# Hybrid decoder step on one core: first weight blocks on a second queue, fewer unread products, and the third block's transposes moved

## The chip, the cores and the metric

The kernel runs on one core of a Trainium2 chip. The metric is the device time of one launch in microseconds. A core has a matrix engine (TensorE, PE in the profile; its weight loads are listed apart as PEld), a vector engine (VectorE, DVE), a scalar engine (ScalarE, ACT), GpSimd (POOL) and SyncE (SP), each with its own instruction stream. In this kernel SP issues most transfers; ScalarE and GpSimd issue some.

## The reference, cut to what matters

The reference is one inference step of a hybrid decoder layer (Mamba-2 and gated linear attention side by side, cross-attention into 256 memory tokens, a convolutional feed-forward part). It serves a prompt of 256 tokens and 8 samples of 4 tokens. The change concerns the first thing the kernel computes, the memory keys and values of the prompt:

```python
def _mem_kv(mem, norm_mem, w_ck, w_cv):
    mn = _rmsnorm(mem, norm_mem)                    # mem: 256 rows of 2048
    k = (mn @ w_ck).reshape(Bsz, N_MEM, CROSS_HEADS, CROSS_HEAD_DIM)
    v = (mn @ w_cv).reshape(Bsz, N_MEM, CROSS_HEADS, CROSS_HEAD_DIM)
```

The first stage of the kernel is one quarter of the first product: the keys of head 0, `mn @ w_ck[:, 0:512]`, a 256 x 2048 matrix times a 2048 x 512 one. The row factor of the norm (`mrs`) is applied at the end of the product, so the stage only has to scale by the gains `norm_mem` before it multiplies.

## The kernel before, in words

The contraction over 2048 is cut into 16 blocks of 128 (`KT`). Every operand is split into a high and a low float32r half, and a product is made of three matmul terms: high x high, low x high, high x low. A weight block of 128 x 512 (256 KB, tile `raw`) is loaded by `wload` (L108), and `wsplit` (L100) makes `whi` with a ScalarE cast (L103) and `wlo` with a VectorE subtraction (L105). Six `raw` tiles are in rotation, five pairs of halves.

The memory rows are loaded two blocks at a time by `mem_load` (L290, 256 KB into `mt`). `mem_prep` (L296) turns one block: two TensorE transposes (L300), then `split_from` (L195), in which ScalarE multiplies by the gain and writes `mn_hi` (L197) and VectorE writes `mn_lo` (L198). The gains come as a row `mrow`, loaded on ScalarE's queue (L285), are turned by one transpose (L374) and copied to `gmem` (L375).

`prep_mem` (L371) calls `mem_prep`, and for every odd block squares one 128 x 512 piece of the rows on ScalarE (L384), with its sum read out, for the row factor; block 15 has two such pieces. So on ScalarE the order within an odd block is gain, square, cast; within an even block gain, cast.

`mem_proj` (L326) puts it together. Its generator `feed` issues the loads of a pair of blocks, prepares each block and splits its weights. Before the loop, `ready` is filled with blocks 0 and 1. In the loop, block `kk` is multiplied with six matmuls of 512 columns (L348, L349 for each half of the rows, then L352), and then `ready` is filled again: with two blocks after block 0, with one after each other block. So the transposes of blocks 2 and 3 stand between the products of blocks 0 and 1, and from then on the transposes of block k+3 stand behind the products of block k.

Two groups of products of a matrix of ones, which nobody reads, stand on TensorE: nine ahead of the stage (L389), six after the transposes of block 1 (L379).

Within this stage the order on TensorE, ScalarE, VectorE and SP is the program's, written out by `tc.manual_schedule` (L385). The rest of the program is ordered by a planner that simulates time (L42); it may move an instruction forward into free places, which is how an instruction of line 533 (`acol`, the exponential of a small vector) and the copies of line 455 (`dcol`) stand among those of this stage. `tc.keep_in_program_order` pins an instruction.

After this stage the same `mem_proj` runs for other heads without `prep`, woven with the preparation of x (L501).

Of the kernel before, what the change touches and what calls it, by code (L numbers as in the profile page):

```python
# [11 lines left out]
ACT = mybir.ActivationFunctionType  # L12
# [4 lines left out]
P = 128  # L17
# [25 lines left out]
def hybrid_step(ctx: ExitStack, tc: tile.TileContext, I: dict, O: list):  # L43
    ctx.enter_context(tc.block(schedule_with_timeline_sim=True))
    nc = tc.nc
    (y_p, y_s, o_pconv, o_pssd, o_pgla, o_pffn, o_pmk, o_pmv, o_sconv, o_sssd, o_sgla, o_sffn) = O
    V, S, G = nc.vector, nc.scalar, nc.gpsimd
# [13 lines left out]
    def acc_tiles(n):  # L61

        turn[0] += 1
        return [ps.tile([P, 512], F32, tag=f"acc{turn[0] % 2}", bufs=2, name="acc") for _ in range(n)]

    def mm_tile():
        return ps.tile([P, 512], F32, tag="mm", bufs=3, name="mm")
# [23 lines left out]
    dcol = const.tile([P, KT], F32, name="dcol")  # L91
    dtb = const.tile([32, 1], F32, name="dtb")
    alog = const.tile([32, 1], F32, name="alog")

    def vec(name):
        o, n = vofs[name]
        return vcol[:, o:o + n]


    def wsplit(raw):  # L100

        hi = wp.tile(list(raw.shape), F32R, tag="whi", bufs=WB, name="whi")
        S.copy(hi, raw)  # L103
        lo = wp.tile(list(raw.shape), F32R, tag="wlo", bufs=WB, name="wlo")
        V.tensor_tensor(lo, raw, hi, ALU.subtract)  # L105
        return hi, lo

    def wload(src):  # L108
        raw = wp.tile([P, src.shape[1], src.shape[2]], F32, tag="raw", bufs=RB, name="raw")
        nc.sync.dma_start(out=raw, in_=src)  # L110
        return raw

    late = []
# [57 lines left out]
    def run(*gens):  # L171
        for g in gens:
            for _ in g:
                pass
# [105 lines left out]
    with pool("p0") as p0:  # L280
# [1 line left out]
        mn_lo = p0.tile([P, KT, SEQ], F32R, name="mn_lo")  # L282
        vrow = p0.tile([P, P], F32, name="vrow")
        mrow = p0.tile([KT, P], F32, name="mrow")
        S.dma_start(out=mrow, in_=I["norm_mem"].rearrange("(t p) -> t p", p=P))  # L285
        S.preload_act_table_set(LNEXP)
        S.copy(epsc[:, 2:3], epsc[:, 0:1])
        mt = p0.tile([P, 9, 512], F32, tag="rows", name="mt")[:, 0:8].rearrange("p (i q) d -> p i (q d)", i=2)
# [1 line left out]
        def mem_load(k0):  # L290
            cs = slice(k0 * P, (k0 + 2) * P)
            nc.sync.dma_start(out=mt[:, :, cs], in_=I["mem_prompt"][0, :, cs].rearrange("(i p) c -> p i c", p=P))
# [33 lines left out]
        def mem_proj(w, hd, dst, prep=None, hold=None):  # L326

            def feed():
                for k0 in range(0, KT, 2):
                    if prep is not None:  # L330
                        mem_load(k0)
                    raws = [wload(w[k * P:(k + 1) * P, 512 * hd:512 * hd + 512].rearrange("(k p) n -> p k n", p=P))
                            for k in (k0, k0 + 1)]
                    for k in range(2):
                        if prep is not None:
                            prep(k0 + k)
                        yield wsplit(raws.pop(0))

            accs = acc_tiles(2)
            ws = feed()  # L340
            ready = [next(ws) for _ in range(2)] if prep is not None else []
            for kk in range(KT):
                if prep is None:
                    ready.append(next(ws))
                hi, lo = ready.pop(0)
                for m in range(2):
                    ms_ = slice(m * P, (m + 1) * P)
                    MM(accs[m], mn_hi[:, kk, ms_], hi[:, 0, :], start=(kk == 0), stop=False)  # L348
                    MM(accs[m], mn_lo[:, kk, ms_], hi[:, 0, :], start=False, stop=False)  # L349
                for m in range(2):  # L350
                    ms_ = slice(m * P, (m + 1) * P)
                    MM(accs[m], mn_hi[:, kk, ms_], lo[:, 0, :], start=False, stop=(kk == KT - 1))  # L352
                if prep is not None:
                    ready += [w_ for w_ in (next(ws, None) for _ in range(2 if kk == 0 else 1)) if w_]
                if turning and next(turning[0], STOP) is STOP:
                    turning.pop(0)
                yield

            def rows():
                t = p0.tile([P, 2, 512], F32, tag="mp", bufs=2, name="mp")  # L360
                for m in range(2):
                    S.activation(t[:, m, :], accs[m], ACT.Identity, scale=mrs[:, m:m + 1])
                G.dma_start(out=dst[0, :, hd, :].rearrange("(m p) d -> p m d", p=P), in_=t)
                if dst is o_pmk:
                    turning.append(key_turn(hd, t))
            if hold is None:
                rows()
            else:
                hold.append(rows)

        def prep_mem(kk):  # L371
            if kk == 0:
                a = mm_tile()
                TR(a[:, 0:KT], mrow, ident[0:KT, 0:KT])  # L374
                V.tensor_copy(gmem, a[:, 0:KT])  # L375
            mem_prep(kk)
            if kk == 1:
                for _ in range(6):
                    MM(wm[:, 0:P], ones, ones, start=True, stop=True)  # L379
            for n in range(kk // 2 - 1 if kk % 2 else 8, kk // 2 + kk // (KT - 1)):  # L380
                if n >= 0:
                    sq = p0.tile([P, 512], F32, name="junk")
                    i, q = n % 2, n // 2
                    S.activation(sq, mt[:, i, q * 512:(q + 1) * 512], ACT.Square, accum_out=mss[:, i, q:q + 1])  # L384
        with tc.manual_schedule(engines={mybir.EngineType.PE, mybir.EngineType.Activation, mybir.EngineType.DVE,  # L385
                                        mybir.EngineType.SP}):
            wm = mm_tile()
            for _ in range(9):
                MM(wm[:, 0:P], ones, ones, start=True, stop=True)  # L389
            run(mem_proj(I["w_ck"], 0, o_pmk, prep_mem, held))  # L390

# [14 lines left out]
        drow = p0.tile([P, 2 * KT], F32, name="drow")  # L406
# [15 lines left out]
        def x_norm():  # L422
            ss = p0.tile([P, 9], F32, name="ss")

            def square(b):
                junk = p0.tile([P, 512], F32, name="junk")
                tc.keep_in_program_order(S.activation(junk, xrow[:, b, :], ACT.Square, accum_out=ss[:, b:b + 1]))
                tc.keep_in_program_order(
                    V.transpose(xT[:, :, 32 * b:32 * b + 32], xrow[:, b, :].rearrange("p (x j) -> p j x", j=KT)))

            for step in range(37):
                if step in (5, 9, 15, 21, 27):
                    x_load((step - 3) // 6)
                if step == 3:

                    V.tensor_reduce(mrs, mss, AX.X, ALU.add)
                    S.activation(mrs, mrs, ACT.Ln, scale=1.0 / D, bias=epsc[:, 0:1])
                    S.activation(mrs, mrs, ACT.Exp, scale=-0.5)
                if step == 6:
                    held.pop()()  # L440
                if step % 3 == 0 and step >= 12:
                    square(step // 3 - 5 if step > 12 else 8)
                yield
            yield
            a = mm_tile()
            TR(a[:, 0:r], vrow[0:r, :], ident[0:r, 0:r])
            TR(a[:, 128:224], crow, ident[0:96, 0:96])
            yield
            V.tensor_copy(vcol[:, 0:r], a[:, 0:r])
            V.tensor_scalar(scw, a[:, 128:224], 0.5, None, ALU.mult)  # L450
            ob, nb_ = vofs["ssd_conv_b"]
            V.tensor_scalar(vcol[:, ob:ob + nb_], vcol[:, ob:ob + nb_], 0.5, None, ALU.mult)
            V.tensor_scalar(rg, vec("gla_norm"), 0.5, None, ALU.mult)
            for e in range(2):
                V.tensor_copy(dcol[64 * e:64 * e + 64, :],
                              drow[64 * e:64 * e + 64, :].rearrange("p (t e) -> p e t", e=2)[:, e, :])
            yield

            dg = p0.tile([P, 9, NS], F32, name="dg")
            V.tensor_tensor(dg, fold4.unsqueeze(1).to_broadcast([P, 9, NS]), ss.unsqueeze(2).to_broadcast([P, 9, NS]), ALU.mult)  # L460
            yield
            a = mm_tile()
            MM(a[:, 0:T], ones, dg.rearrange("p c t -> p (c t)"), start=True, stop=True)
            S.activation(rtok, a[:, 0:T], ACT.Ln, scale=1.0 / D, bias=epsc[:, 0:1])
            S.activation(rtok, rtok, ACT.Exp, scale=-0.5)
# [45 lines left out]
        acol = p0.tile([32, 1], F32, name="acol")  # L511
# [18 lines left out]
        run(proj_w(dt_load, 112, X, KT, dt_cons))  # L530

        def dt_prep():
            S.activation(acol, alog, ACT.Exp)
            S.activation(dte, dtx, ACT.Abs)
            S.activation(dte, dte, ACT.Exp, scale=-1.0)
            S.activation(dte, dte, ACT.Ln, bias=1.0)
# [1191 lines left out]
    for i in range(5):  # L1728
        src = I["ffn_conv_w"][i] if i < 3 else I["ffn_conv_b"] if i == 3 else I["norm_final"]
# [266 lines left out]
```

## Time and profile before

| what | value |
|---|---|
| median of 3 runs | 2477.01 us (2476.76 to 2479.82) |
| the profiled execution, its own time | 2480.01 us |
| its span, first to last instruction | 2478.3 us |
| TensorE busy | 2464.7 us, 99% of the span |
| VectorE, ScalarE, GpSimd busy | 1774.8, 1354.7, 439.4 us |
| moved by DMA | 530.77 MB, 214 GB/s on average |

The first stage takes the first 33 us or so of this span. A row of a time line has the start, the duration, the engine, the line and operation, the tile written and the tiles read, and a count; in brackets stands how long the engine idled before it and what released it. "SPq" and "ACTq" are issues of transfers from SP and ScalarE. Durations of matmuls overlap, since they are pipelined: the distance between starts is their rate.

### The profile page before, as it was taken

The page shows a single profiled execution, that of the slowest core. Times are in us where ns is not written, and L with a number is a line of the kernel's source. Part 1 is how long each engine was busy: PE and PEld are TensorE (multiplying, and loading weights), DVE is VectorE, ACT ScalarE, POOL GpSimd, SP SyncE. Part 2 cuts the span into 40 slices and gives each one's busy share as a digit, 9 for nine tenths or more (in the row PEclk, how much of TensorE's full clock was granted, in tenths as well). Part 3 has the DMA queues.
Part 4 walks back from the last instruction along what each step waited for, and adds up shares of the span by engine and source line. Part 5 has one row for each costly group of instructions (what it writes and reads, how often), then busy time and mean ns, then how long its engine had stood idle before and what let it go on. Part 6 is the DMA issues. An engine that isn't in the chain of part 4 may idle for free.

```text
span 2478.3 us, 52123 instructions
## 1 busy us (share of the span) xinstructions
PE 2464.7 (99%) x18738; PEld 2385.7 (96%) x18738; DVE 1774.8 (72%) x3804; ACT 1354.7 (55%) x2781; POOL 439.4 (18%) x798
## 2 busy tenths in 40 slices
PE   9999999999999999999999999999999999999998
PEld 7889999999999999999999998999999999999998
DVE  6866778796877666777666676667777676776766
ACT  6765657646464655544455554565545454554545
POOL 3103144252111010110111122402101001010012
PEclk9999999999999999999999999999999999999999
DMA  8878687777769685877777698656555555555555
GB/s 259 258 237 236 175 261 210 224 224 227 218 210 297 198 262 184 244 254 221 233 232 256 199 355 308 198 165 174 168 172 171 171 168 177 167 174 169 170 172 168
DMA packets 457652, 530.77 MB, mean 214 GB/s; under 512 B 40316, under 2 KB 403676, under 8 KB 457360
## 3 DMA queue, kind: packets, MB, share of 16 engines
q1 hardware_dynamic: 420272, 422.39, 56.4%
q0 software_dynamic: 37088, 105.03, 13.2%
q8 instruction: 147, 2.41, 0.4%
q14 instruction: 113, 0.93, 0.1%
q10 hardware_dynamic: 32, 0.01, 0.0%
HBM read 476.41 MB, written 50.86 MB: 213 GB/s over the span
## 4 chain that ended last, share of the span: by engine, by line
PE 96%; DMA 2%; DVE 1%; POOL 1%; ACT 0%; issue 0%; SPq 0%; DVEq 0%; POOLq 0%; ACTq 0%
PE acc L149 27%; PE acc L148 27%; PE acc L153 27%; PE acc L348 2%; PE acc L352 2%; PE acc L349 2%; DMA raw<-in_w_in_dram 1%; POOL sqr L777 1%; PE mm L1260 1%; PE la L1251 1%; PE la L1603 1%; PE la L1661 1%; PE mm L1215 0%; DMA vc<-in_cache_mem_v_dram 0%; PE la L926 0%
## 5 line engine op out<-in xcount | busy, mean ns | idle before, releaser
L103 ACT CAST whi<-raw 128x512 fp32r<-128x512 f32 x1464 | 898.3, 618 | 951.4 <-PE acc L149 805.1
L105 DVE TENSOR_TENSOR wlo<-raw,whi 128x512 fp32r<-128x512 f32 x1464 | 994.3, 686 | 532.5 <-ACT whi L103 522.4
L149 PE MATMUL acc<-xn,whi 128*128 128x288 f32 (+1 forms) x1936 | 540.8, 295 | 0.0
L148 PE MATMUL acc<-xn,whi 128*128 128x288 f32 (+1 forms) x1936 | 539.6, 294 | 0.2 <-ACT whi L103 0.2
L153 PE MATMUL acc<-xn,wlo 128*128 128x288 f32 (+1 forms) x1936 | 407.9, 293 | 0.0
L149 PE MATMUL acc<-hf,whi 128*128 128x288 f32 x1408 | 393.2, 296 | 0.0
L148 PE MATMUL acc<-hf,whi 128*128 128x288 f32 x1408 | 388.6, 292 | 0.0
L148 PEld LDWEIGHTS acc<-xn,whi 128*128 128x128 f32 (+1 forms) x1936 | 363.4, 188 | 5.6 <-issue 3.5
L149 PEld LDWEIGHTS acc<-xn,whi 128*128 128x128 f32 (+1 forms) x1936 | 363.7, 188 | 3.1
L153 PEld LDWEIGHTS acc<-xn,wlo 128*128 128x128 f32 (+1 forms) x1936 | 309.8, 188 | 0.5 <-DVE wlo L105 0.2
L153 PE MATMUL acc<-hf,wlo 128*128 128x288 f32 x1408 | 294.5, 290 | 0.0
L149 PEld LDWEIGHTS acc<-hf,whi 128*128 128x128 f32 x1408 | 264.5, 188 | 0.0
L148 PEld LDWEIGHTS acc<-hf,whi 128*128 128x128 f32 x1408 | 264.0, 188 | 0.0
L153 PEld LDWEIGHTS acc<-hf,wlo 128*128 128x128 f32 x1408 | 226.3, 188 | 0.1
L149 PE MATMUL acc<-pr,whi 128*128 128x288 f32 x704 | 196.5, 295 | 0.0
L148 PE MATMUL acc<-pr,whi 128*128 128x288 f32 x704 | 194.7, 293 | 0.0
L1777 POOL COPY fsp<-fst 128x16 f32<-128x16 f32 x88 | 36.2, 413 | 653.6 <-DVE av L1789 371.3
L153 PE MATMUL acc<-pr,wlo 128*128 128x288 f32 x704 | 147.3, 290 | 0.0
L148 PE MATMUL acc<-un,whi 128*128 128x288 f32 x512 | 143.1, 295 | 0.3 <-DVE ma L1031 0.3
L149 PE MATMUL acc<-un,whi 128*128 128x288 f32 x512 | 143.0, 295 | 0.0
L149 PEld LDWEIGHTS acc<-pr,whi 128*128 128x128 f32 x704 | 132.3, 188 | 0.0
L148 PEld LDWEIGHTS acc<-pr,whi 128*128 128x128 f32 x704 | 132.0, 188 | 0.0
(564 smaller groups left out, 4316.6 us busy)
## 6 DMA issues: line engine op xcount, KB each, us to landing
raw<-in_w_in_dram SPq DMA_DIRECT2D x480, 256.0 KB, 3.9
raw<-in_w_up_dram SPq DMA_DIRECT2D x352, 256.0 KB, 2.8
raw<-in_w_down_dram SPq DMA_DIRECT2D x176, 256.0 KB, 2.9
raw<-in_w_ck_dram SPq DMA_DIRECT2D x64, 256.0 KB, 5.2
raw<-in_w_cv_dram SPq DMA_DIRECT2D x64, 256.0 KB, 4.5
raw<-in_w_ssd_out_dram SPq DMA_DIRECT2D x64, 256.0 KB, 3.5
sin<-in_state_gla_dram POOLq DMA_DIRECT2D x32, 512.0 KB, 6.4
out_dram<-sin SPq DMA_DIRECT2D x32, 512.0 KB, 3.7
```

The lines of the kernel that those rows point to most:

```text
L103: S.copy(hi, raw)
L105: V.tensor_tensor(lo, raw, hi, ALU.subtract)
L148: MM(a, hi[:, k, cs], xh, start=(k0 + s0 + k == 0), stop=False)
L149: MM(a, hi[:, k, cs], xl, start=False, stop=False)
L153: MM(a, lo[:, k, cs], xh, start=False, stop=(k0 + s0 + k == nk - 1))
L348: MM(accs[m], mn_hi[:, kk, ms_], hi[:, 0, :], start=(kk == 0), stop=False)
L349: MM(accs[m], mn_lo[:, kk, ms_], hi[:, 0, :], start=False, stop=False)
L352: MM(accs[m], mn_hi[:, kk, ms_], lo[:, 0, :], start=False, stop=(kk == KT - 1))
L777: tc.keep_in_program_order(G.dma_start(out=sq_[32 * i:32 * i + 32].rearrange("p (r d) -> p r d", d=32), in_=rows[i]))
L1251: MM(osa[NS * j:NS * j + NS, :], qdm[:, k, b, :], sins[b][:, k, :], start=False, stop=(q == 1 and k == 0))
L1260: MM(a, kb[:, k * P:(k + 1) * P], vst, start=True, stop=True)
L1777: G.tensor_copy(sp[:, :, 0:2], st.rearrange("p (b k) -> p b k", k=2))
```

## The change

Six edits, all in what runs first or is pinned:

1. `wload` takes an engine. The first two weight blocks of `w_ck` are loaded by ScalarE's queue (`first`), at the place where the gain row was loaded.
2. The gain row is loaded by SP, after the first memory rows.
3. The memory rows of blocks 2 and 3 are loaded directly after it, ahead of all other weight blocks; the later order is unchanged.
4. The unread products are five and two instead of nine and six.
5. The pair of blocks that was prepared after the products of block 0 is not prepared there. Block 2 is prepared within block 1, after the first two of its matmuls, and block 3 at the end of block 1; from then on one block after each block, as before.
6. The copies to `dcol` and the exponential to `acol` are pinned to the program's order.

```diff
-    def wload(src):
+    def wload(src, eng=None):
         raw = wp.tile([P, src.shape[1], src.shape[2]], F32, tag="raw", bufs=RB, name="raw")
-        nc.sync.dma_start(out=raw, in_=src)
+        (eng or nc.sync).dma_start(out=raw, in_=src)
...
-        S.dma_start(out=mrow, in_=I["norm_mem"].rearrange("(t p) -> t p", p=P))
+        first = [wload(I["w_ck"][k * P:(k + 1) * P, 0:512].rearrange("(k p) n -> p k n", p=P), S) for k in range(2)]
...
                 for k0 in range(0, KT, 2):
-                    if prep is not None:
+                    if prep is not None and k0 != 2:
                         mem_load(k0)
-                    raws = [wload(w[k * P:(k + 1) * P, 512 * hd:512 * hd + 512].rearrange("(k p) n -> p k n", p=P))
-                            for k in (k0, k0 + 1)]
+                    if prep is not None and k0 == 0:
+                        nc.sync.dma_start(out=mrow, in_=I["norm_mem"].rearrange("(t p) -> t p", p=P))
+                        mem_load(2)
+                        raws = first
+                    else:
+                        raws = [wload(w[k * P:(k + 1) * P, 512 * hd:512 * hd + 512].rearrange("(k p) n -> p k n", p=P))
+                                for k in (k0, k0 + 1)]
...
                     MM(accs[m], mn_lo[:, kk, ms_], hi[:, 0, :], start=False, stop=False)
+                    if prep is not None and kk == 1 and m == 0:
+                        ready.append(next(ws))
...
-                if prep is not None:
-                    ready += [w_ for w_ in (next(ws, None) for _ in range(2 if kk == 0 else 1)) if w_]
+                if prep is not None and kk:
+                    ready += [w_ for w_ in (next(ws, None),) if w_]
...
             if kk == 1:
-                for _ in range(6):
+                for _ in range(2):
                     MM(wm[:, 0:P], ones, ones, start=True, stop=True)
...
-            for _ in range(9):
+            for _ in range(5):
                 MM(wm[:, 0:P], ones, ones, start=True, stop=True)
...
-                V.tensor_copy(dcol[64 * e:64 * e + 64, :],
-                              drow[64 * e:64 * e + 64, :].rearrange("p (t e) -> p e t", e=2)[:, e, :])
+                tc.keep_in_program_order(V.tensor_copy(
+                    dcol[64 * e:64 * e + 64, :], drow[64 * e:64 * e + 64, :].rearrange("p (t e) -> p e t", e=2)[:, e, :]))
...
-            S.activation(acol, alog, ACT.Exp)
+            tc.keep_in_program_order(S.activation(acol, alog, ACT.Exp))
```

## Prediction

> **What bounds the kernel now.** I read the page first, then the waits of TensorE, then the time lines of TensorE, ScalarE and the SP queue over the first 33 us, because the change touches nothing later.
>
> ```profile
> span 2478.3 us, 52123 instructions
> PE 2464.7 (99%) x18738; PEld 2385.7 (96%) x18738; DVE 1774.8 (72%) x3804; ACT 1354.7 (55%) x2781; POOL 439.4 (18%) x798
> ...
> PE 96%; DMA 2%; DVE 1%; POOL 1%; ACT 0%; issue 0%; SPq 0%; DVEq 0%; POOLq 0%; ACTq 0%
> ...
> PE la L1661 <- DMA vc<-in_cache_mem_v_dram: 1.3, 1, 1.3
> ...
> PE mm L300 <- DMA mt<-in_mem_prompt_dram: 0.6, 1, 0.6
> ```
>
> TensorE is busy for 99% of the span and makes 96% of the chain that ended last, so a microsecond won or lost on TensorE at the beginning is a microsecond at the end. The list of TensorE's waits (total, times, longest) shows how little is left to win: the longest one, far behind the change, and one for the memory rows. What the beginning can also win is time in which TensorE is busy with products nobody reads; the busy share doesn't tell those apart, the time line does (start, duration, count).
>
> ```profile
> 1.13 3.83 PE L389 MATMUL mm<-ones 128*128 128x128 f32 x18 [1.13 <-DVE epsc L78]
> 4.90 0.23 PE L374 MATMUL mm<-ident,mrow 16*128 16x16 f32 x1
> 5.06 0.44 PE L300 MATMUL mm<-ident,mt 128*128 128x128 f32 x2
> ...
> 5.55 1.50 PE L379 MATMUL mm<-ones 128*128 128x128 f32 x12
> 6.81 0.48 PE L348 MATMUL acc<-whi,mn_hi 128*128 128x512 f32 x1
> ...
> 9.05 0.44 PE L300 MATMUL mm<-ident,mt 128*128 128x128 f32 x2 [0.60 <-DMA mt<-in_mem_prompt_dram]
> ...
> 9.46 0.48 PE L348 MATMUL acc<-whi,mn_hi 128*128 128x512 f32 x1
> ...
> 11.32 0.48 PE L348 MATMUL acc<-whi,mn_hi 128*128 128x512 f32 x1
> ```
>
> Nine unread products (18 instructions) run from 1.13; the transposes of blocks 0 and 1 from 5.06; six more unread products from 5.55; the products of block 0 from 6.81. Then TensorE waits for the second load of memory rows, transposes blocks 2 and 3 at 9.05, and does the products of block 1 from 9.46 and of block 2 from 11.32. From there it doesn't wait in this stage. The measure of the new beginning is therefore the start of block 2's products, now 11.32.
>
> **The first part: the new beginning.** Who lets block 0 and block 2 start is seen on the queues.
>
> ```profile
> 0.82 0.46 SPq L292 DMA_DIRECT2D mt<-in_mem_prompt_dram  x1
> 1.34 0.93 SPq L110 DMA_DIRECT2D raw<-in_w_ck_dram  x2
> ...
> 2.31 6.69 DMA mt<-in_mem_prompt_dram
> ...
> 0.81 0.44 ACTq L285 DMA_DIRECT2D mrow<-in_norm_mem_dram  x1
> 1.29 1.28 ACT L286 ACT_TABLE_LOAD   x1 [1.29 <-PEq L1984]
> ...
> 5.53 0.47 ACT L197 ACTIVATE mn_hi<-mm,gmem 128x256 fp32r<-128x256 f32 x1 [2.76 <-PE mm L300]
> 5.91 0.61 ACT L103 CAST whi<-raw 128x512 fp32r<-128x512 f32 x1
> ...
> 9.89 0.61 ACT L103 CAST whi<-raw 128x512 fp32r<-128x512 f32 x1
> ...
> 3.00:4.00 1.00, 1.00 (x6) 1.00 (x6) 1.00 (x2) 0.00 (x0) 1.00 (x5) 1.00 1.11 323
> ```
>
> Unread products. Eighteen instructions become ten, twelve become four. The first ten end at about 1.13 + 10 x 0.21 = 3.3 (3.83 / 18 = 0.21 each), so TensorE is free for the transposes from 3.3 instead of 4.90. But the transposes need the gains (mrow) and the first rows, and the trace doesn't say when these land, only that both were there by 4.90 and 5.06. The change puts mrow behind the rows on SP and lets the first weight block run beside the rows. The last row above is a stretch of 1 us in which all queues moved 323 GB/s: one more transfer of 262 KB served in between delays the rows by at most 0.8 us. So the transposes of block 0 start between 3.3 (all landed early) and 5.06 + 0.8 = 5.9. I take 5.4, half of the delay on top of 5.06: four 256 KB transfers took until 9.00, and no row shows an early landing. From there ScalarE decides: the first transposes start at 5.06 and the cast of the first weight block ends at 5.91 + 0.61 = 6.52, 1.46 us later. The products of block 0 start at 5.4 + 1.5 = 6.9. Two unread products (4 instructions of (6.81 - 5.55) / 12 = 0.11, 0.44 in all) fit in between and cost nothing. Block 0 takes six products, 1.4 us (below), so block 1 starts at 8.3 and, after its first two products, the transposes of block 2 come at 8.8.
>
> Loads. The rows of blocks 2 and 3 (issued at 2.31, landed at 9.00) are now SP's third transfer, about 0.5 us earlier. The bytes ahead of and beside them stay the same, four times 256 KB. I take 8.5 for the landing (bounds 7.5 and 9.0); at 8.8 nobody waits for them, at 9.0 it costs 0.2.
>
> ScalarE issues two transfers instead of one before its table load, 0.5 us more; its next work is due at 5.53, the table load ends at 2.57, so this is covered by over 2 us. The later weight blocks are issued two places earlier on SP; nothing is queued behind them that TensorE needs sooner.
>
> Block 2's products need its cast. From the transposes at 9.05 to the end of that cast at 9.89 + 0.61 = 10.50 were 1.45 us; from 8.8 that gives 10.25, and TensorE's own path (four products, one transpose pair) gives 10.1. So block 2 starts at 10.26 in place of 11.32: **a gain of 1.06 us.**
>
> The clock. The same 128-column instruction is slow early and fast later, which the granted clock of the windows (1.00 throughout) doesn't show:
>
> ```profile
> L389 PEld LDWEIGHTS mm<-ones x18: 192/333/338, 1.1 to 4.6; 128*128 128x128 f32 x18
> ...
> L379 PEld LDWEIGHTS mm<-ones x12: 190/192/192, 5.4 to 6.7; 128*128 128x128 f32 x12
> ```
>
> TensorE ran at about half speed until some 3.3 us after its first product. Now it works for 2.1 us, pauses for about as long, and does transposes. Either full speed comes anyway (0), or 3.3 us after the transposes at 5.4, at 8.7 (1.8 us of products at half speed, costing 0.9), or 3.3 us after block 0 starts (1.65). I take 0.5, nearer to no cost, because in this trace the pause from 8.3 to 9.05 left the speed alone. The net gain of the beginning is 1.06 - 0.5 = **0.56 us**.
>
> **The second part: one block less in hand.** Before, block 0's products were followed by the transposes of two blocks, and from then on the transposes of block k+3 stood behind the products of block k. The change drops the pair after block 0 and inserts one block's transposes inside block 1; at its end comes one more. From there the transposes of block k+2 stand behind the products of block k: only one block of products now covers transposes, ScalarE's gain and cast. Here is block 7 of before, its transposes, its work on ScalarE, and the products.
>
> ```profile
> 16.02 0.38 PE L300 MATMUL acc<-ident,mt 128*128 128x128 f32 x2
> 16.16 0.48 PE L348 MATMUL acc<-whi,mn_hi 128*128 128x512 f32 x1
> ...
> 17.63 0.38 PE L300 MATMUL mm<-ident,mt 128*128 128x128 f32 x2
> 17.77 0.48 PE L348 MATMUL acc<-whi,mn_hi 128*128 128x512 f32 x1
> ...
> 19.37 0.47 PE L348 MATMUL acc<-whi,mn_hi 128*128 128x512 f32 x1
> ...
> 16.44 0.47 ACT L197 ACTIVATE mn_hi<-acc,gmem 128x256 fp32r<-128x256 f32 x1 [0.64 <-PE acc L300]
> 16.81 0.62 ACT L384 ACTIVATE junk<-mt 128x512 f32<-128x512 f32 x1
> 17.34 0.19 ACT L384 ACTIVATION_READ_ACCUMULATOR junk<-mt 128x1 f32 x1
> 17.43 0.61 ACT L103 CAST whi<-raw 128x512 fp32r<-128x512 f32 x1
> ...
> 18.42 0.61 ACT L103 CAST whi<-raw 128x512 fp32r<-128x512 f32 x1
> ```
>
> Transposes at 16.02, products of blocks 5 and 6 at 16.16 and 17.77, its own at 19.37: two blocks of cover. ScalarE handed over the cast at 17.43 + 0.61 = 18.04, which is 2.02 us after the transposes began, because every odd block has a square (0.62 and its read) between gain and cast. With one block of cover the products would be due 17.77 - 16.02 = 1.75 us after the transposes. They wait 2.02 + 0.04 - 1.75 = 0.31 us (0.04 is what the gain at 16.44 starts behind the transposes' end at 16.40). An even block has no square: 18.42 + 0.61 - 17.63 = 1.40 us, under 1.75, no wait. The odd blocks 5, 7, 9, 11 and 13 pay 0.31 each, 1.55. Block 3, whose transposes stand late in block 1 (9.92 by the sum above), gets its cast at 9.92 + 2.06 = 11.98 and is due at about 11.80: 0.18. Block 15 has two squares:
>
> ```profile
> 29.08 0.38 PE L300 MATMUL acc<-ident,mt 128*128 128x128 f32 x2
> ...
> 31.25 1.12 ACT L103 CAST whi<-raw 128x512 fp32r<-128x512 f32 x2
> ...
> 30.69 0.40 PE L348 MATMUL acc<-whi,mn_hi 128*128 128x512 f32 x1
> ...
> 32.08 0.39 PE L348 MATMUL acc<-whi,mn_hi 128*128 128x512 f32 x1
> ...
> 11.89 0.20 ACT L533 ACTIVATE acol<-alog 32x1 f32<-32x1 f32 x1
> ...
> L105 DVE TENSOR_TENSOR wlo<-raw,whi 128x512 fp32r<-128x512 f32 x1464 | 994.3, 686 | 532.5 <-ACT whi L103 522.4
> ```
>
> Its first cast ends about 31.25 + 0.61 = 31.86, 2.78 us after its transposes began; the products would be due 1.61 us after them (30.69 - 29.08, one block with no transposes behind it; a block is 32.08 - 30.69 = 1.39): 2.78 + 0.04 - 1.61 = 1.21. **Loss: 1.55 + 0.18 + 1.21 = 2.94 us.** Bounds: nothing (if something I don't see moves the squares) to 3.2 (if the waiting instruction costs a further 0.04 each time). VectorE's remainder (0.69, the last row) isn't late: it is read by the fifth product, 4 x 1.39 / 6 = 0.93 us later.
>
> The two pins (acol and dcol) move one ScalarE instruction of 0.20 us, which stood at 11.89 among the casts, and two small VectorE copies to later places where both engines have idle time; nothing.
>
> **The sum.** 2.94 - 0.56 = +2.4 us on TensorE. The profiled execution took 2480.01 us, 1.7 above its span, and 3.0 above the median of the three runs; the added 2.4 gives 2482.4 for it, and for the median 2477.01 + 2.4 = **2479.4 us**. A planner orders the rest of the program; a shift of its start may swap neighbours there. The waits that TensorE shows behind the change, the largest 1.3 us, are the size I give that, on either side. About 0.2% (5 us) is what a measurement of this kernel can tell from no change, and the forecast lies inside it.
>
> **The rivals.**
>
> Rival one, the cover is enough: ScalarE's squares slip into its idle time, no odd block waits, and only the beginning counts: -0.56 to -1.06, or with early rows (transposes at 4.5, 0.9 sooner) -1.96; time 2476.0. For it: ScalarE idled 0.64 us before each odd gain (the row at 16.44). Against: the order on ScalarE is written out, and the wait comes out of four consecutive rows.
>
> Rival two, the second queue brings nothing: rows delayed by the full 0.8, transposes at 5.9, block 2 at 10.8: a gain of 0.56 before the clock, so +2.9, 2479.9. For it: the transfers were close to the rate limit from 3.00 to 4.00. Against: the rows stand first on their queue.
>
> The Trainium skill, page "DMA: Bandwidth & Descriptors", section "Issuing engines are not separate DMA queues", speaks for this rival and against the change: transfers of all queues interleave on the same engines, and a second queue saves only the time of issuing. By it the sum is the rival's 2479.9; no row here has two bulk queues at once, so the trace can't yet agree or differ.
>
> Rival three, slower by over 0.2%: TensorE stays at half speed. Place: block 0 onward. Price: half of the stretch. Without a clock term the sum is 2.94 - 1.06 = 1.88; block 3's wait is hidden then, 1.70. It decides from 3.3 us of price, a stretch of 6.6 us, two of the 3.3 us that the trace needed; three give 2477.0 + 1.7 + 5.0 = 2483.7. For it: 2.1 us of unread work followed by a pause of the same length. Against: the real products are dense as soon as they start.
>
> The Trainium skill, "TensorE: Matmul & The Clock Gate", section "Part 1: The HAM clock gate", has full speed come after about 3.4 us of sustained work, counted in windows that run freely. The trace agrees with its length (3.3 us); by the page a busy start that stops at 3.3 us may miss the window, and one missed window would cost up to 1.7 us.
>
> **How the numbers follow.** Forecast (the cover is short): 0.58. Rival one 0.22, rival two 0.13, rival three 0.07. The likeliest gives 2479.4. The low end takes in rival one with a microsecond of the planner's, 2475.0; the high end the forecast with one missed window (1.2 more than taken) and about as much of the planner's, 2482.4. Faster by over 0.2% needs 5 us, more than the beginning holds: 0.02. Slower by over 0.2%: rival three and a tail of the forecast, 0.10. Within: 0.88.
>
> **What would show it.** Right: in the changed profile block 2's products start near 10.3; TensorE waits on ScalarE's cast about 0.3 us for each odd block from 5 and 1.2 us for block 15; the stage ends about 2.4 us later. Wrong: no wait on the casts (rival one), rows landing after 9 (rival two), load instructions of over 300 ns beside the products of blocks 0 to 2 (rival three), or a difference of the total that arises behind 33 us.

## The result, and the profile after

| | median | lowest to highest | runs |
|---|---|---|---|
| before | 2477.95 us | 2476.75 to 2481.60 | 22 |
| changed | 2482.85 us | 2480.73 to 2484.79 | 22 |

The ratio is 1.0018, with a 95% interval of 1.0011 to 1.0025: the changed kernel is slower by about 4.5 us (2.7 to 6.2; the two medians of the table differ by 4.9). The prediction was 2479.4, with a range from 2475.0 to 2482.4, so the median lies 0.45 us above its high end. The profiled execution of the changed kernel took 2482.41 us. From its page, in the order of the lines shown for before:

```profile
span 2480.7 us, 52090 instructions
...
PE 2464.8 (99%) x18722; PEld 2385.0 (96%) x18722; DVE 1775.3 (72%) x3804; ACT 1354.2 (55%) x2781; POOL 439.9 (18%) x798
...
PE 96%; DMA 1%; POOL 1%; DVE 1%; ACT 0%; issue 0%; DVEq 0%; SPq 0%; ACTq 0%; POOLq 0%
```

Eight unread products, sixteen instructions, are gone (18738 to 18722). The span grew by 2.4 us and TensorE's busy time by 0.1, but that sum hides two opposite moves. Up to the start of block 2's products TensorE is busy for 8.37 us in place of 9.53, because products are gone and it waits instead. From there to the second block of the next product it is busy for 25.42 us in place of 23.50, although only one pair of transposes is added (the weight loads grow from 19.08 to 19.41): the row of a pipelined matmul reaches past the start of the next one, so that a short wait behind it still counts as busy. The distances between starts show such waits, the busy time doesn't. The time line of TensorE in the changed kernel:

```profile
1.14 2.50 PE L396 MATMUL mm<-ones 128*128 128x128 f32 x10 [1.14 <-DVE epsc L78]
5.44 0.25 PE L381 MATMUL mm<-ident,mrow 16*128 16x16 f32 x1 [1.80 <-DMA mrow<-in_norm_mem_dram]
5.62 0.69 PE L300 MATMUL mm<-ident,mt 128*128 128x128 f32 x2
...
6.53 1.06 PE L386 MATMUL mm<-ones 128*128 128x128 f32 x4
7.38 0.80 PE L353 MATMUL acc<-whi,mn_hi 128*128 128x512 f32 x1
...
9.40 0.39 PE L353 MATMUL acc<-whi,mn_hi 128*128 128x512 f32 x1
...
9.86 0.38 PE L300 MATMUL mm<-ident,mt 128*128 128x128 f32 x2
...
11.31 0.50 PE L353 MATMUL acc<-whi,mn_hi 128*128 128x512 f32 x1
```

TensorE now waits 1.80 us for the gain row instead of doing unread products. Block 0 starts at 7.38 (before 6.81) and takes 2.02 us, to 9.40, instead of 1.4. Block 2 starts at 11.31, where it started at 11.32: the new beginning has won nothing. The weight loads of TensorE, with shortest, median and longest duration, show a second reason, half speed:

```profile
L386 PEld LDWEIGHTS mm<-ones x4: 333/333/337, 6.3 to 7.0; 128*128 128x128 f32 x4
L353 PEld LDWEIGHTS acc<-whi,mn_hi x4: 188/239/330, 7.4 to 10.0; 128*128 128x128 f32 x4
```

They take 333 ns until 7.0, and the first of block 0 still up to 330: full speed came amid block 0. The cover is seen at block 7, on TensorE and on ScalarE:

```profile
18.15 0.38 PE L300 MATMUL acc<-ident,mt 128*128 128x128 f32 x2
18.29 0.48 PE L353 MATMUL acc<-whi,mn_hi 128*128 128x512 f32 x1
...
19.76 0.38 PE L300 MATMUL mm<-ident,mt 128*128 128x128 f32 x2
20.22 0.50 PE L353 MATMUL acc<-whi,mn_hi 128*128 128x512 f32 x1
```

```profile
18.57 0.48 ACT L197 ACTIVATE mn_hi<-acc,gmem 128x256 fp32r<-128x256 f32 x1 [0.99 <-PE acc L300]
18.95 0.62 ACT L391 ACTIVATE junk<-mt 128x512 f32<-128x512 f32 x1
19.46 0.19 ACT L391 ACTIVATION_READ_ACCUMULATOR junk<-mt 128x1 f32 x1
19.56 0.61 ACT L103 CAST whi<-raw 128x512 fp32r<-128x512 f32 x1
```

The products of block 7 start 0.46 us behind the next transposes (20.22 - 19.76) instead of 0.14: a wait of 0.32, ended by the cast at 19.56 + 0.61 = 20.17. The list of waits, on the side of TensorE's weight loads, puts six together: 0.17 before block 2, 0.31 before each of blocks 5, 7, 9 and 11, and the longest before block 15, seen also in the time line. Block 13 isn't in the list, but its products stand at the same distance from the transposes (30.44 to 30.89).

```profile
PEld acc L353 <- ACT whi L103: 2.9, 6, 1.5
```

```profile
35.21 0.50 PE L353 MATMUL acc<-whi,mn_hi 128*128 128x512 f32 x1 [1.04 <-ACT whi L103]
...
38.06 0.39 PE L353 MATMUL acc<-whi,mn_hi 128*128 128x512 f32 x1
```

The last row, the second block of the next product, is the mark that I use for the end of the stage; before it stood at 34.82.

### The profile page after: what moved, and what is told of

It reads as the page before. It is cut to its first block, busy times and chain, and to the rows that moved or that the text cites. A ratio compares the mean times of both kernels' runs of the same rounds, so it can differ in the third digit from the quotient of the medians.

```text
span 2480.7 us, 52090 instructions
## 1 busy us (share of the span) xinstructions
PE 2464.8 (99%) x18722; PEld 2385.0 (96%) x18722; DVE 1775.3 (72%) x3804; ACT 1354.2 (55%) x2781; POOL 439.9 (18%) x798
## 4 chain that ended last, share of the span: by engine, by line
PE 96%; DMA 1%; POOL 1%; DVE 1%; ACT 0%; issue 0%; DVEq 0%; SPq 0%; ACTq 0%; POOLq 0%
PE acc L149 28%; PE acc L148 27%; PE acc L153 27%; PE acc L353 2%; PE acc L354 2%; PE acc L359 2%; POOL sqr L784 1%; PE mm L1267 1%; PE la L1258 1%; PE la L1610 1%; PE la L1668 1%; PE mm L1222 0%; DMA vc<-in_cache_mem_v_dram 0%; DMA raw<-in_w_in_dram 0%; PE la L933 0%
```

## The experiments

Two marks of each profile make the stage comparable: the start of block 2's products, which measures the beginning, and from there to the second block of the next product, which measures the rest of the stage. In us:

| kernel | block 0 | block 2 | end mark | block 2 to end | ratio to before (95%) |
|---|---|---|---|---|---|
| before, first and second profile | 6.81, 7.89 | 11.32, 11.33 | 34.82, 34.80 | 23.50, 23.47 | |
| changed, first and second profile | 7.38, 7.36 | 11.31, 11.44 | 38.06, 38.18 | 26.75, 26.74 | 1.0018 (1.0011 to 1.0025) |
| e1 cover | 7.47 | 12.47 | 36.08 | 23.61 | 1.0008 (0.9999 to 1.0016) |
| e2 squares last | 7.28 | 11.62 | 35.38 | 23.76 | 1.0009 (1.0000 to 1.0018) |
| e3 nine unread | 7.38 | 10.80 | 37.53 | 26.73 | 1.0011 (1.0002 to 1.0020) |
| e4 transposes alone | 6.89 | 10.26 | 36.97 | 26.71 | 1.0014 (1.0005 to 1.0023) |
| e5 loads alone | 7.40 | 10.83 | 34.32 | 23.49 | 1.0000 (0.9991 to 1.0009) |
| e6 unread alone | 5.57 | 11.30 | 34.80 | 23.50 | 0.9997 (0.9988 to 1.0006) |
| e7 pins alone | 7.32 | 10.76 | 34.37 | 23.61 | 1.0000 (0.9991 to 1.0009) |
| e8 before, mid | 7.25 | 10.66 | 34.41 | 23.75 | 1.0000 (0.9991 to 1.0009) |
| e9 changed, mid | 6.69 | 10.20 | 33.95 | 23.75 | 1.0000 (0.9992 to 1.0009) |
| e10 before, mid, five | 5.59 | 9.86 | 33.62 | 23.76 | 0.9998 (0.9990 to 1.0007) |
| e11 changed, squares twice | 7.71 | 12.46 | 45.28 | 32.82 | 1.0051 (1.0037 to 1.0065) |
| e12 before, squares twice | 7.25 | 10.68 | 35.79 | 25.11 | 1.0009 (1.0000 to 1.0018) |
| e13 before, delayed | 6.72 | 10.79 | 37.83 | 27.04 | 1.0012 (1.0003 to 1.0021) |

The interval of one experiment is about 2 us to either side. The ratios rank the large effects; the marks, which repeat within about 0.15 us from block 2 on in kernels with the same cover, tell the rest.

**The theory and its rivals.** Theory A: the cover of one block is too short for the odd blocks, that costs 3 us, and half speed in the beginning costs the rest. Theory B: a good part of the loss arises behind the stage. A third possibility was that it is not the cover but ScalarE's own time.

**e1: the cover restored in the changed kernel.**

```diff
-                    ready += [w_ for w_ in (next(ws, None),) if w_]
+                    ready += [w_ for w_ in (next(ws, None) for _ in range(2 if kk == 1 else 1)) if w_]
```

> The changed kernel with one edit: after block 1 two blocks are prepared instead of one (3 and 4), so that from there the transposes of block k+3 stand behind the products of block k, as before the change. Theory A (the short cover costs about 3 us in the stage; the rest of the loss is the beginning at half speed): no wait on the casts of the odd blocks, about 2.9 us less than the changed kernel, so 1 to 2 us above the kernel before (ratio 1.0004 to 1.0008). Theory B (half of the loss arises behind the stage, from a planner's order or other transfers): the waits go, but the ratio stays at 1.0012 or more.

Measured: 1.0008. The waits of TensorE's weight loads up to 37 us hold no cast any more:

```profile
PEld mm L381 <- issue: 2.2, 1, 2.2
PEld mm L396 <- DVE epsc L78: 1.1, 1, 1.1
```

and from block 2 to the end mark it takes 23.61, as before. What is left lies ahead of block 2, which starts only at 12.47, because in this execution half speed lasted through the first weight loads of block 1:

```profile
L353 PEld LDWEIGHTS acc<-whi,mn_hi x3: 288/331/331, 7.5 to 9.8; 128*128 128x128 f32 x3
```

**e2: the squares behind the cast.** The square of an odd block is moved from between gain and cast to behind the cast; the cover stays one block.

```diff
-                        yield wsplit(raws.pop(0))
+                        done = wsplit(raws.pop(0))
+                        if prep is not None:
+                            prep_squares(k0 + k)
+                        yield done
...
+        def prep_squares(kk):
```

> The changed kernel with ScalarE's squares behind the cast of the block instead of between its gain and its cast; the cover stays one block. Theory A: the cast of an odd block is ready about 1.4 us after its transposes begin, like an even one, under the 1.75 at which it is due: no wait, about 2.9 us less than the changed kernel, as with the longer cover. If it is the missing block itself and not the square between gain and cast, the odd blocks still wait about 0.3 us each and the time stays at 1.0018 of before.

Measured: 1.0009, and one wait of 0.2 us, at block 2, is left of the six:

```profile
PEld acc L356 <- ACT whi L103: 0.2, 1, 0.2
```

So it was the square between gain and cast that didn't fit into one block of cover. The 23.76 from block 2 on is 0.26 longer than before: one pair of transposes (0.23), block 4's, that before stood ahead of block 2's products and now stands behind them.

**e3: nine unread products ahead in the changed kernel.**

```diff
-            for _ in range(5):
+            for _ in range(9):
```

> The changed kernel with nine unread products ahead of the stage again instead of five (the second group stays at two). Theory A: TensorE runs until 4.9 us, the load instructions of block 0 take 190 ns instead of 330, block 0 is done about 0.9 us sooner in the profile, and the time falls by 0.5 to 1.5 us against the changed kernel (ratio 1.0012 to 1.0016). Theory B: the beginning doesn't matter for the total, 1.0018 stays. If the clock needs more than 3.3 us whatever runs, the loads of block 0 stay at 330 ns.

Measured: 1.0011, just below the expected 1.0012 to 1.0016. The weight loads of the products have full speed from block 0 on, and block 2 starts 0.5 us sooner than in the changed kernel's first profile; the cover's loss is untouched (26.73).

```profile
L353 PEld LDWEIGHTS acc<-whi,mn_hi x5: 186/187/188, 7.4 to 10.8; 128*128 128x128 f32 x5
```

**e4: the fifth edit alone, in the kernel before.** (The moved `next(ws)` and the condition `kk`, as in the diff of the change.)

> The kernel before with the fifth edit alone: no blocks prepared after block 0, block 2's transposes within block 1, block 3's at its end. Loads and unread products as before. Theory A: block 2 starts about 0.8 us sooner (10.5 instead of 11.32, the rows still land at 9.0), the odd blocks wait 0.3 us each and block 15 1.2: 2.1 us above before (ratio 1.0009). Theory B: under 1 us above before.

Measured: 1.0014, above the 1.0009 expected but with it inside the interval. Block 2 starts at 10.26, 1.06 us sooner, and the rest of the stage takes 3.2 longer, so that the end mark is 2.15 us later. The rows did not hold it to 9.0: block 2's transposes ran at 8.81 without a wait. The waits are the changed kernel's:

```profile
PEld acc L348 <- ACT whi L103: 2.9, 6, 1.5
```

**e5, e6 and e7: the other edits alone, in the kernel before.** e5 has the two loads on ScalarE's queue, the gain row and the early rows on SP; e6 has five and two unread products; e7 the two pins.

> The kernel before with the loads alone changed: first two weight blocks on ScalarE's queue, gain row and memory rows of blocks 2 and 3 early on SP. Unread products 9 and 6, cover of two blocks, as before. Theory A: the gain row lands at 5.3 instead of before 4.9, block 0 starts 0.4 us later (7.2), the rows of blocks 2 and 3 are there by 8.6, block 2 starts 0.4 us sooner than 11.32: within 1 us of before (ratio 0.9996 to 1.0002). If the second queue brings real speed, block 0 and block 2 start 1 us sooner or more. If the transfers only get in each other's way, block 2 starts at 12 or later.

> The kernel before with five and two unread products instead of nine and six, nothing else. Theory A (half speed in block 0 costs): the transposes run as soon as gains and rows land, at 4 to 4.9, but block 0 has load instructions of 330 ns and takes 2 to 2.8 us instead of 1.4, and how long depends on the run; since the rows of blocks 2 and 3 land at 9.0 anyway, 0 to 1 us above before (ratio 1.0000 to 1.0005), with a lowest time above that of before. Theory B (unread products are pure loss): 0.5 us or more below before.

> The kernel before with the sixth edit alone: acol and dcol pinned to the program's order. Theory A: neither engine is late where they now stand, 1.0000 within the interval. Theory B (half of the loss arises behind the stage): the exponential now stands among the casts of a later projection, and the ratio is 1.0005 or more.

Measured: none differs from before by anything that can be told (1.0000, 0.9997, 1.0000), and from block 2 to the end mark all three take 23.5 to 23.6. e5: block 0 at 7.40, block 2 at 10.83; Theory A's expectation held. The second queue shows no higher peak rate: the best 1 us up to 10 us is 400 GB/s in e5, 384 and 383 in the two profiles of before and 396 in e7, which has the old loads. The Trainium skill's page "DMA: Bandwidth & Descriptors" ("Issuing engines are not separate DMA queues") has transfers of all queues interleave on the same engines. e5 agrees with that in its peak. What the new order of loads does is to fill a dip, from 4 to 5 us (360 GB/s against 216 and 279), and that brought no time. e6's expected loss didn't come, but the run tells something that no profile of before could:

```profile
3.57 0.28 PE L374 MATMUL mm<-ident,mrow 16*128 16x16 f32 x1
3.81 0.69 PE L300 MATMUL mm<-ident,mt 128*128 128x128 f32 x2
...
9.01 0.44 PE L300 MATMUL mm<-ident,mt 128*128 128x128 f32 x2 [1.44 <-DMA mt<-in_mem_prompt_dram]
```

With the old loads, gains and first rows are there by 3.57 and 3.81; with the changed loads TensorE waited for the gain row until 5.44, and in the other profiles with these loads until 5.33 to 5.77. So the new order of loads made the gain row about 1.8 us later or more, and fewer unread products could then not be turned into an earlier start. In e6 itself the early start ended in a wait of 1.44 us for the rows of blocks 2 and 3.

**e11 and e12: every square twice.** The second square writes the same values as the first.

```diff
-                    S.activation(sq, mt[:, i, q * 512:(q + 1) * 512], ACT.Square, accum_out=mss[:, i, q:q + 1])
+                    for _ in range(2):
+                        S.activation(sq, mt[:, i, q * 512:(q + 1) * 512], ACT.Square, accum_out=mss[:, i, q:q + 1])
```

> The changed kernel with every square done twice (the second overwrites the first with the same values), so 0.71 us more on ScalarE between the gain and the cast of each odd block, two of them in block 15. Theory A (the cover is one block, used up): each of the odd blocks waits 0.7 us more, block 15 1.4 more; 7 x 0.71 = 5.0 us above the changed kernel, 1.0036 to 1.0042 of before. If ScalarE's time is covered, under 1 us.

> The kernel before with every square done twice, 0.71 us more on ScalarE for each odd block and 1.4 for block 15. Theory A: with two blocks of cover only block 15, with 0.2 us to spare, waits, 1.2 us, and the other odd blocks don't: 1 to 1.5 us above before (1.0004 to 1.0007), where the changed kernel lost 9.5 us by the same addition. If ScalarE's time itself is what the stage lacks and not the cover, 4 us or more.

Measured: the changed kernel 1.0051, the kernel before 1.0009. The same 5 to 6 us of work on ScalarE lengthens the stage from block 2 on by 6.1 us in the changed kernel (26.75 to 32.82) and by 1.6 in the kernel before (23.50 to 25.11), nearly all of it at block 15. The waits up to 48 us, of the changed kernel with double squares and then of the kernel before with double squares:

```profile
PEld acc L353 <- ACT whi L103: 9.1, 8, 3.0
```

```profile
PEld acc L348 <- ACT whi L103: 1.6, 1, 1.6
```

ScalarE's time is covered with two blocks in hand and laid bare with one. That e11 lost 13.8 us by its median, and not the 9.4 expected, has several parts in its profile. The expectation counted seven squares, and there are eight: one each in blocks 3 to 13, two in block 15, none in block 1. Block 2 started 1.1 us later than in the changed kernel's first profile. And at 60 us a wait of 3.0 us for `wlo` came, because ScalarE and VectorE had stood for over 3 us waiting for rows of x (until 58.5); whether the longer stage brought that about is not shown.

**e13: a pure delay in the kernel before.** Two unread products behind each of blocks 4 to 11.

```diff
+                if prep is not None and 4 <= kk < 12:
+                    for _ in range(2):
+                        MM(delay[:, 0:P], ones, ones, start=True, stop=True)
...
+            delay = la_tile()
```

> The kernel before with nothing but a delay of the same size as the waits on the casts: sixteen unread products of 0.21 us, two after each of blocks 4 to 11, 3.4 us of TensorE time. Theory A (a microsecond of the stage is a microsecond at the end, and the rest of the 4.4 us is chance and the clock): 3.4 us above before, ratio 1.0012 to 1.0015. Theory B (what comes behind the stage makes a delay larger): 1.0018 or more. If the rest of the kernel absorbs delays, 1.0008 or less.

Measured: 1.0012, 3.1 us by the medians of the same chip, for 3.5 us in the stage. The median fits a delay that arrives at the end as it is; the interval (0.7 to 5.2 us) is too wide to show it alone. The profiles say more. From the end mark to the last instruction it takes 2443.5 and 2442.0 us in the two profiles of before, 2442.6 and 2442.2 in those of the changed kernel, and 2442.5 in e13. What lies behind the stage thus takes no longer in the changed kernel, and Theory B has no support left; e7 is nothing as well.

**The two kernels once more.**

> The changed kernel once more, one profile. Theory A: the odd blocks wait the same 0.3 us as in the first profile, but TensorE comes to full speed at another moment than at 8.3 us, so that block 2 starts at another time than 11.31 (10.3 to 12.5).

> The kernel before once more, one profile. Its first profiled execution was 2.0 us above its median: if that lies in chance waits behind the stage, the waits at the value loads near 1546 us and around 560 us are shorter here, and block 2 starts within 0.3 us of 11.32 again, because the rows of blocks 2 and 3 set it and not the clock.

The changed kernel: block 2 at 11.44, 26.74 from there. The kernel before: 2478.55 us; block 2 at 11.33, though for another reason than I expected: here half speed lasted through the first unread group and past it, the second group then ended late, and block 0 started at 7.89. Its weight loads were at full speed from block 0 on:

```profile
L348 PEld LDWEIGHTS acc<-whi,mn_hi x4: 188/189/192, 7.9 to 10.0; 128*128 128x128 f32 x4
```

The wait of 1.3 us for the value rows near 1546 us is gone, as is the one of 0.5 on `qe`: the first profiled execution of before, 2.1 us above its median, had waits that belong to that execution and not to the kernel.

**e8, e9 and e10: can it be made faster?** e8 is the kernel before with block 2's transposes within block 1, the squares behind the casts and nine and two unread products. e9 is the changed kernel with the gain row first on ScalarE's queue, nine unread products and the squares behind the casts. e10 is e8 with five and two.

> The kernel before with block 2's transposes within block 1 and block 3's at its end, the squares behind the casts, nine and two unread products; loads as before. Theory A: block 0 starts at 6.6, full speed throughout, block 2 starts at about 10.3 (rows landing by 8.8 to 9.0), no odd block waits: about 1 us below before (ratio 0.9994 to 0.9998). If the order inside block 1 is itself what costs, it is not below before.

> The changed kernel with the gain row first on ScalarE's queue, nine unread products ahead, and the squares behind the casts. Theory A (the second queue brings nothing for the rate): block 0 starts at 6.6 to 7.1, block 2 at 10.0 to 10.5, the same as the kernel that keeps the loads of before, within 0.5 us (ratio 0.9994 to 0.9999). If the second queue helps, block 2 starts at 9.6 or sooner and it is 0.5 us or more below that kernel.

> The kernel before with block 2's transposes within block 1, the squares behind the casts, and five and two unread products, loads as before. Theory A: block 0 is done by 7 to 8, half of block 1 runs before the rows of blocks 2 and 3 land at 8.8 to 9.0, block 2 starts at 10.3 to 10.5 in place of 11.3 and no odd block waits: 0.8 us below before, 0.9996, which the measurement can't tell from no change; its lowest time is below before's lowest.

Measured: 1.0000, 1.0000 and 0.9998. All three avoid the waits (23.75 from block 2 on). e10 has the earliest block 2 of all (9.86), and its ratio to before lies 0.0020, 5 us, below the changed kernel's; against the kernel before no difference can be told. e8 and e9 missed their gain of a microsecond in the totals. In the profile of e9 a wait of 1.2 us for `wlo`, between 86 and 88 us, is of the size of what the stage had won; e8's stage was only 0.4 us shorter.

## Why the prediction was wrong, point by point

**What held.** The loss by the lost cover was predicted at 2.94 us, from four rows of ScalarE in the profile of before. Its steps are in the changed profile: 0.31 to 0.32 at blocks 5 to 13 (predicted 0.31), 0.12 at block 3 (0.18), 1.2 at block 15 (1.21). e1 and e2 take it away in two different ways, e4 brings it alone, e11 and e12 double its cause. Shown, not argued. The pins cost nothing that can be told, as said. Rival one fell with the waits. The second queue did bring no time, as rival two has it; in the profiles of the changed beginning the transposes start at 5.52 to 5.96, between the forecast's 5.4 and that rival's 5.9 or a little past it. Rival three, slower by over 0.2%, is not what the ratio says (0.18%), but the sign named for it came: weight loads of 330 ns beside the products of block 0.

**What failed is the first part, "The net gain of the beginning is 1.06 - 0.5 = 0.56 us".** Two of its terms were mis-sized, and one more was missing from the second part.

- The half speed: "I take 0.5, nearer to no cost, because in this trace the pause from 8.3 to 9.05 left the speed alone". A pause at full speed says nothing about coming to full speed. In the changed kernel's two profiles it came amid block 0, and in those of e1 and e11, with the same beginning, in block 1. It cost 0.26 between the transposes and the gain behind them (the gain began 0.73 us after the transposes, before 5.53 - 5.06 = 0.47) and 0.6 in block 0: 0.9 us where it came early, and about 0.8 us more where it came late (12.24 in e1 and 12.46 in e11 against 11.31, less the 0.1 and 0.3 by which the transposes were later). These are the two prices that the prediction had listed, 0.9 and 1.65; it was wrong to lean towards none. With nine unread products full speed came between 4.3 and about 7 us in the profiles, with five between 6.3 and over 10. The Trainium skill ("TensorE: Matmul & The Clock Gate", "Part 1: The HAM clock gate") counts the work in windows of about 3.4 us that run freely. The traces agree in so far as the moment moves, by less than one such window (about 2.5 us between the two profiles of before), while the kernel stays the same.
- The measure: block 2's start was compared with its start in one profile, 11.32. Among five profiles with the beginning of before (before twice, e7, e12, e13) it is 11.32, 11.33, 10.76, 10.68 and 10.79, on average 10.98. Among five with the changed beginning (changed twice, e1 less 0.23 for the pair of transposes it has ahead, e2, e11) it is 11.31, 11.44, 12.24, 11.62 and 12.46, on average 11.81. The beginning doesn't gain 0.56 us, it loses about 0.8 by these averages. The forecast put block 2's start at 11.32 - 0.56 = 10.76: the average of the changed beginning is 1.05 later, and that of before 0.34 sooner than the start it was compared with.
- One pair of transposes, 0.23 us, was not counted: before, block 4's transposes stood ahead of block 2's products. So block 2 to the end mark grew by 3.25 and not by 2.94.

With these terms the change costs 0.84 + 3.25 = 4.1 us of TensorE, 1.7 more than the 2.4 forecast (1.05 + 0.34 + 0.31), and the ratio gives about 4.5 (2.7 to 6.2). What remains between them can't be told from chance. How the 0.84 divides between half speed and the later gain row is known for single profiles only.

**The baseline.** I added the loss to the median of three runs, 2477.01; over 22 runs it is 2477.95. That alone is twice the distance by which the median left the range. The high end allowed for "the forecast with one missed window and about as much of the planner's", and had nothing in it for the spread of before: with the later median of before the same loss of 2.4 us would have given 2480.3.

**The start at 5.4** came out at 5.62, but not for the reason given. "No row shows an early landing" was true only because TensorE was busy until 4.90; e6 shows the data there by 3.81. The gain row's delay behind the rows and beside the weights is not 0.8 but about 1.9 us or more (5.44 - 3.57), so that fewer unread products left TensorE waiting.

## What to carry to other kernels

When a step is moved nearer to its use, write down what every other engine must do in between, one period long, and compare it with the time that is left; the rows for that stand in the profile of the kernel before. Unread products ahead of a stage are not waste to be cut as long as the data aren't there, and cutting them can pay only if the data come early too. A start that depends on the clock has to be read from several profiles, since one shows one moment out of a range of some us.

## What the runs showed of the hardware that I had not expected

The moment of full speed moved from execution to execution of the same beginning by about 2.5 us (about 4.5 and about 7 in the two profiles of before), while from block 2 on the stage repeated to 0.03 us (23.50 and 23.47; 26.75 and 26.74). And a small transfer of 8 KB, put behind 256 KB on one queue while two transfers of 256 KB ran on a second, came 1.9 us later than when it went first on that second queue, or more (5.44 and 5.42 against 3.57 or sooner); 0.5 us of that is its later issue (1.34 against 0.81).
